# The router's logits with the weights held still, the last column block's idle products, and the end of the last norm, in a Hymba block on one core

## The chip, the core and the metric

The kernel runs on one core of a Trainium2 chip. The metric is the time of one execution in device microseconds (us). The core has TensorE (PE, with its weight load PEld), VectorE (DVE), ScalarE (ACT), GpSimd (POOL) and SyncE (SP), which issues most of the DMAs.

## What is computed

```python
def block(x, c, ...):                     # x: 512 tokens x 2048 columns
    shift, scale, gate, shift2, scale2, gate2 = split(silu(c) @ w_ada + b_ada)
    h  = rmsnorm(x) * (1 + scale) + shift
    oa, ob = swa_attention(h @ w_in), fox_attention(h @ w_in)
    x1 = x + gate * (concat(rmsnorm(oa), rmsnorm(ob)) @ w_out)
    h2 = rmsnorm(x1) * (1 + scale2) + shift2
    logits = h2 @ [w_group | w_expert]    # 4 groups and 32 experts: 36 columns
    # top-1 of 4 groups, then top-2 of the 8 experts of that group
    x2 = x1 + gate2 * moe(h2)
    return rmsnorm(x2, final_g)
```

Products that decide the router are made in full fp32, or as three products of split halves (hi*hi, lo*hi, hi*lo).

## The kernel before

The tokens are four blocks of 128 (`tb`). The part that the change touches first is the output projection. x1 is made in four blocks of 512 columns, `cc`, in the order 2, 0, 1, 3. For a block, 16 pieces of w_out (512 KB each; two of one kind in `n`, `j`) are loaded by SP (L360) into a ring of five buffers named `raw`; ACT rounds a piece to `hi_s` (L175), DVE makes the remainder `lo_s` (L176), and PE does for each half piece twelve products into four accumulators `oq` (L214 to L216, three for each token block). The first loop over `cc` has slots only for half pieces 4 to 6, block 3 for all; the last piece of a block is done in `out_last`, token block by token block, with DVE's `gx` and `x` after each (L1108, L1109: x1 = x + gate * accumulator).

Beside it runs `ada_side`: four sections of w_ada for the last gate (`gm`), eight loads of 512 KB each, in the same `raw` ring, with the same SP queue. Half of a section's tiles go through DVE (`ga`, L621), half through ACT (L623, scales the buffer in place) and POOL (L624, adds it to `gb`). Its steps are written out at a fixed rate, 66 for 26 half pieces.

The third thing between output products is the `Tail` of a block that is done. For a token block it is a T step (`tr`: four transposes of x1 into PSUM, `x1T`, L1123; ACT squares x1 for the norm, L1116, and copies x1T to `x1Ts`, L1127) and an L step (`logit`: four fp32 products with x1Ts held and the 36 router columns `wr` streamed, L1132, each two PE instructions, and one DVE operation that adds the result `lp` to `lg`, L1134 and L1136). `steps()` yields T and L in turn, eight steps for a block; the loop takes one step after each half piece with `next(steps, 0)`. There are 24 steps for the blocks 2, 0 and 1, and 23 slots; the rest is done before the last piece. PSUM tag `t`, in which x1T, lp and `gr` (the ada side's transposed result, L596) live, has two buffers.

The last block, 3, has its T and L steps in `out_last` and after it, on a PSUM tile of its own (`lp4`). Then DVE adds lg and lp4 (L1199), multiplies by the norm's factor rs (L1211), adds the bias (L1212), and a chain of some twenty small operations chooses groups and experts, up to `chosen_b` (L1253). In that time PE does `turn(22)`, 22 products of the identity with itself into a tile that nobody reads (L1229, fp32, two instructions each); then `rk` (ranks, L1257), `turn(8)`, and the gather `xe` (L1499) of the first expert pair, whose DVE and ACT work follows (L1480, L1486, L1506, L1508). 16 expert pairs follow, 1024 KB of weights a load.

The end is `last_norm`: the squares of x2, by five chunks of columns (four of them 512, 512, 512, 256 and the last 256 wide) for each token block, on ACT (L1605) into `sf5`; DVE reduces (L1608), scales (L1609), takes the inverse root with ACT's help (L130 to L134), and writes the output in eight halves of 1024 columns (L1616), each sent by SP (L1617).

Of the kernel before, what the change touches and what calls it, by code (L numbers as in the profile page):

```python
# [8 lines left out]
F32 = mybir.dt.float32  # L9
# [3 lines left out]
AF = mybir.ActivationFunctionType  # L13
OP = mybir.AluOpType
AX = mybir.AxisListType

T = 512
D = 2048
TB = 4
EPS = 1e-6  # L20
# [33 lines left out]
def kernel(  # L54
# [8 lines left out]
    V, S, G, PE, SP = nc.vector, nc.scalar, nc.gpsimd, nc.tensor, nc.sync  # L63
# [8 lines left out]
    def bcast(v, n):  # L72
        return bass.AP(tensor=v.tensor, offset=v.offset, ap=[[0, 128], [1, n]])
# [5 lines left out]
    def flat(t):  # L79
        return t.rearrange("p a b -> p (a b)")  # L80
# [18 lines left out]
    ident = big.tile([128, 128], F32, name="ident")  # L99
# [408 lines left out]
    def bank(shape, name):  # L508

        return pb["pool"].tile(shape, F32, tag=pb["tag"], name=name, bufs=pb["bufs"])  # L510
# [328 lines left out]
    def side_step():  # L839
        f = side_late.pop(0) if side_late else None  # L840
        if f:
            f()

    def attend(segs):


        us = [(u, i) for i, sg in enumerate(segs) for u in sg[0]]
        counts = [sum(1 for _, j in us if j == i) for i in range(len(segs))]
        late, at = None, -1
        for k in range(len(us) + LAG):  # L850
            u, i = us[k] if k < len(us) else (None, len(segs) - 1)
            if i != at:
                if at >= 0:
                    fill.drain()
                at = i
                _, make, total, hook = segs[i]
                fill = make()
                step = total / (2.0 * counts[i] + (2.0 * LAG if i == len(segs) - 1 else 0.0))
                if hook:
                    hook(fill)  # L860
                if u.pre:
                    u.pre()
                    fill.take(1.3)
            if u:
                u.a1()
            if 0 < k <= len(us):
                us[k - 1][0].a2()
            fill.take(step)
            if late:
                late()  # L870
                late = None
            if k >= LAG:
                us[k - LAG][0].b()
                late = us[k - LAG][0].c
            fill.take(step)
            if k + 1 < len(us) and us[k + 1][1] == at and us[k + 1][0].pre:
                us[k + 1][0].pre()
            else:
                side_step()
        late()  # L880
        return fill
# [19 lines left out]
    for g in range(4):  # L901
        VP += natural(256, lambda g=g: accs("accv", f"vb{g}"),
                      lambda tb, o, g=g: S.activation(vbs[g][:, tb, :], o, AF.Copy))

    def fills(i):
        for kind, n, *to in FILLS[i]:
            if kind == "v":
                for v in VP[n:to[0]]:
                    yield from v
            else:  # L910
                yield from (queries2 if kind == "q" else heads2)(n)
# [84 lines left out]
    wrf = wr.rearrange("p c j e -> p (c j) e")  # L996
# [27 lines left out]
    def more_o(fill):  # L1024
# [3 lines left out]
    total = lambda i: 2.56 * sum(to[0] - n if to else 8 for _, n, *to in FILLS[i])  # L1028
    last6 = list(fox_units((6,), qks, vbs))
    f = attend([  # L1030
        (swa_units(((0, 2), (1, 3), (4, 6), (5, 7))[i]) if i < 4 else
         fox_units((i - 4,), qks, vbs) if i < 10 else last6[:LAST], lambda i=i: Fill(fills(i), side, RATE), total(i),
         hooks.get(i))
        for i in range(11)
    ] + [(last6[LAST:] + list(fox_units((7,), qks, vbs)), lambda: Fill(out_first()), LAST_FILL, router)])
# [20 lines left out]
    mo = ctx.enter_context(tc.tile_pool(name="mo", bufs=1, reuse_waits="tile"))  # L1056
    gm = mo.tile([128, D], F32, name="gm")
    ss2 = mo.tile([128, TB, 4], F32, name="ss2")
    lg = mo.tile([128, TB, 36], F32, name="lg")

    def sm(shape, name, dt=F32):
        return mo.tile(shape, dt, name=name)

    def bc(t, shape):
        return t.to_broadcast(shape)

    rs = sm([128, TB], "rs")
# [23 lines left out]
    class Tail:  # L1091
# [35 lines left out]
            S.activation(self.xT[tb], t, AF.Copy)  # L1127

        def logit(self, tb):
            lp = self.lp4[:, tb, :] if self.last else bank([128, 36], f"lp_{self.cc}_{tb}")  # L1130
            for j in range(4):
                PE.matmul(lp, self.xT[tb][:, j, :], wrf[:, self.cc * 4 + j, :], start=j == 0, stop=j == 3)  # L1132
            if self.cc == 2:
                V.tensor_copy(lg[:, tb, :], lp)  # L1134
            elif not self.last:
                V.tensor_add(lg[:, tb, :], lg[:, tb, :], lp)  # L1136

        def steps(self):
            for tb in range(TB):
                self.tr(tb)  # L1140
                yield
                self.logit(tb)
                yield

    def out_last(t):
# [16 lines left out]
    tail = Tail(2, oacc[2])  # L1162
# [3 lines left out]
    for cc, first in ((0, 4), (1, 4), (3, 0)):  # L1166
        steps = chain(steps, tail.steps())
        ops = []
        for i in range(4):
            k = bank6 % 6  # L1170
# [3 lines left out]
        tail = Tail(cc, ops)  # L1174
# [21 lines left out]
    tail.logit(2)  # L1196
    rms_x1()
    tail.logit(3)
    V.tensor_add(lg, lg, tail.lp4)  # L1199
    pst.close()  # L1200
    frt.close()

# [5 lines left out]
    pb["pool"], pb["tag"], pb["bufs"], hold[0] = ps, "y", 4, True  # L1208
    while side_late:
        side_step()  # L1210
    V.tensor_mul(lg, lg, bc(rs[:, :, None], [128, TB, 36]))  # L1211
    V.tensor_add(lg, lg, bc(brt[:, None, :], [128, TB, 36]))  # L1212

    def one_hot(v, n, mx_, name):
# [11 lines left out]
    def turn(n):  # L1226

        for _ in range(n):
            PE.matmul(idle[:, :128], ident, ident, start=True, stop=True)  # L1229

    turn(22)
    gl = lg[:, :, 0:4]
    gmax = sm([128, TB], "gmax")
    V.tensor_reduce(gmax, gl, axis=AX.X, op=OP.max)
# [20 lines left out]
    for tb in range(TB):  # L1255
        for k in range(tb + 1):
            PE.matmul(rk[:, tb, :], before if k == tb else ones_b, chosen_b[:, k].rearrange("p g e -> p (g e)"),  # L1257
                      start=k == 0, stop=k == tb)
    turn(8)
    place = sm([128, TB, 4, 8], "place")  # L1260
    pf = place.rearrange("p t g e -> p t (g e)")
    V.scalar_tensor_tensor(place, chosen_b, FAR, bc(off.rearrange("p a b e -> p (a b) e")[:, None], [128, TB, 4, 8]),
                           op0=OP.mult, op1=OP.add)
# [19 lines left out]
    HID = cw[:, 5120:5632]  # L1283
# [4 lines left out]
    YT = [cw[:, 5632:6144], more_f[:, 1, :], big.tile([128, 512], F32, tag="wr", name="yt2"), HID]  # L1288
# [225 lines left out]
    def total(tb):  # L1514

        if not x2s:
            x2s.extend(rp_.tile([128, D], F32, tag=f"x2{i}", name=f"x2_{i}") for i in range(TB))
        return x2s[tb]
# [77 lines left out]
    sf5 = sm([128, TB, 5], "sf5")  # L1596
    sf, rf, tf = sm([128, TB], "sf"), sm([128, TB], "rf"), sm([128, TB], "tf")

    def last_norm(cols, tb=0):
        if cols is None:  # L1600
            SP.dma_start(fg, bcast(final_g, D))
            return
        c0, c1 = cols
        i = CHUNKS.index(cols)
        S.activation(HID[:, :c1 - c0], total(tb)[:, c0:c1], AF.Square, accum_out=sf5[:, tb, i:i + 1])  # L1605
        if c1 < D or tb < 3:
            return
        V.tensor_reduce(sf, sf5, axis=AX.X, op=OP.add)  # L1608
        V.tensor_scalar(sf, sf, 1.0 / D, EPS, op0=OP.mult, op1=OP.add)  # L1609
        rsqrt_(rf, sf, tf)  # L1610
        for tb in range(TB):
            y = ring_tile()
            for h in range(2):
                sl = slice(h * 1024, (h + 1) * 1024)
                yv = flat(y)[:, sl]
                V.scalar_tensor_tensor(yv, total(tb)[:, sl], rf[:, tb:tb + 1], fg[:, sl], op0=OP.mult, op1=OP.mult)  # L1616
                SP.dma_start(out[tb * 128:(tb + 1) * 128, sl], yv)  # L1617
# [113 lines left out]
```

## Time and profile before

| | |
|---|---|
| runs of the kernel before | 1891.93, 1893.37, 1896.53 us; median 1893.37 |
| the profiled execution | 1895.8 us; span in the trace 1893.9 us |
| PE busy | 1810.1 us, 96% of the span |
| DVE, ACT, POOL busy | 1018.6, 748.7, 288.2 us |
| DMA | 573.84 MB, mean 303 GB/s |

The span is cut by the trace: output projection 768 to 891 us, router 891 to 906, expert pairs to 1868, end to 1893.9. In the trace "PE L216 MATMUL oq" is line 216 on TensorE writing the tile oq; "[0.38 <-DVE chosen_b]" is idle time before an instruction and what ended it; PEclk is the granted TensorE clock as a share of full speed (1.00 is 2.4 GHz, 0.50 is 1.2 GHz).

### The profile page before, as it was taken

What the parts mean: (1) busy time and instruction counts of PE and PEld (TensorE: products, weight loads), DVE (VectorE), ACT (ScalarE), POOL (GpSimd) and SP (SyncE); (2) the same over time, 40 slices, a digit from 0 to 9 for tenths busy, and PEclk for the clock granted to TensorE, in tenths of its full rate; (3) what the DMA queues carried; (4) which work ended last, traced back from release to release, by engine and by line L of the source; (5) the groups of instructions that cost most, each with busy time, mean ns of one, the idle gap of its engine ahead of it and who ended that gap; (6) DMA issues with size and microseconds to landing.
All of it is one profiled execution on the core that took longest, in us unless ns stands there. A gap on an engine that the chain in (4) does not pass through costs nothing.

```text
span 1893.9 us, 26581 instructions
## 1 busy us (share of the span) xinstructions
PE 1810.1 (96%) x10045; PEld 1131.1 (60%) x10045; DVE 1018.6 (54%) x1812; ACT 748.7 (40%) x1462; POOL 288.2 (15%) x217
## 2 busy tenths in 40 slices
PE   7998999899899999999999999999999999999995
PEld 5668887787787777778544454444444444444432
DVE  4334676666566545757555454544554545545435
ACT  3235656565555443345523233232322323323213
POOL 0000434443354321445000000000000000000000
PEclk8998999999999999999999999999999999999998
DMA  9984555565566342668989999999999999999995
GB/s 338 352 274 106 169 164 152 165 196 173 160 186 186 113 142 78 208 214 295 369 344 397 420 419 421 421 420 420 420 418 421 416 420 420 419 420 416 420 413 215
DMA packets 208791, 573.84 MB, mean 303 GB/s; under 512 B 22624, under 2 KB 110728, under 8 KB 159888
## 3 DMA queue, kind: packets, MB, share of 16 engines
q1 hardware_dynamic: 207744, 572.00, 80.3%
q8 instruction: 81, 1.33, 0.3%
q14 instruction: 54, 0.44, 0.1%
q10 hardware_dynamic: 912, 0.07, 0.0%
HBM read 567.82 MB, written 4.19 MB: 302 GB/s over the span
## 4 chain that ended last, share of the span: by engine, by line
PE 74%; DMA 8%; ACT 7%; DVE 7%; issue 3%; POOL 1%; SPq 0%; DVEq 0%; ACTq 0%; POOLq 0%
PE pu L1363 12%; PE pg L1363 11%; PE y L1385 9%; PE xe L1499 7%; PE o L1407 5%; DMA w<-in_w_up_dram 4%; PE qp L214 3%; PE qp L216 3%; PE qp L215 3%; DMA raw<-in_w_ada_dram 2%; PE gv L325 2%; PE acc L214 1%; PE acc L215 1%; PE acc L216 1%; PE ob L826 1%
## 5 line engine op out<-in xcount | busy, mean ns | idle before, releaser
L1363 PE MATMUL pu<-w,cw 128*64 128x512 f32 x1024 | 239.3, 593 | 4.7 <-DMA w<-in_w_up_dram 4.7
L1363 PE MATMUL pg<-w,cw 128*64 128x512 f32 x1024 | 235.5, 598 | 1.3 <-ACT cw L1508 0.8
L1508 ACT ACTIVATE cw<-xe,shM,scM 128x128 f32<-128x128 f32 x128 | 58.5, 458 | 429.2 <-PE xe L1499 396.2
L1385 PE MATMUL y<-w,more_f 128*64 128x512 f32 x960 | 214.2, 598 | 4.1 <-ACT xp_whi L1480 2.3
L1506 DVE TENSOR_SCALAR cw<-xe,scM,shM 128x128 f32<-128x128 f32 x128 | 52.4, 410 | 299.3 <-ACT cw L1508 299.3
L624 POOL TENSOR_TENSOR gb<-gb,raw 128x512 f32<-128x512 f32 x112 | 162.1, 1448 | 275.8 <-ACT raw L623 211.4
L1410 DVE SCALAR_TENSOR_TENSOR x<-o,wpair,x 128x512 f32<-128x512 f32 x240 | 163.2, 743 | 19.3 <-PE o L1407 19.3
L1363 PEld LDWEIGHTS pu<-w,cw 128*64 128x64 f32 x1024 | 76.0, 137 | 154.1 <-issue 140.3
L1480 ACT ACTIVATE xp_whi<-x,rs 128x256 fp32r<-128x256 f32 x236 | 162.6, 762 | 0.9 <-DVE rs L134 0.9
L1385 PEld LDWEIGHTS y<-w,more_f 128*64 128x64 f32 x960 | 71.2, 137 | 134.4 <-issue 111.1
L1363 PEld LDWEIGHTS pg<-w,cw 128*64 128x64 f32 x1024 | 69.7, 136 | 133.5 <-issue 128.4
L176 DVE TENSOR_TENSOR wlo_s<-raw,whi_s 128x512 fp32r<-128x512 f32 x96 | 91.4, 953 | 107.7 <-ACT whi_s L175 107.6
L1486 DVE SCALAR_TENSOR_TENSOR xp_wlo<-x,rs,xp_whi 128x256 fp32r<-128x256 f32 x232 | 144.8, 681 | 2.2 <-ACT xp_whi L1480 2.2
L621 DVE SCALAR_TENSOR_TENSOR ga<-raw,csil,ga 128x512 f32<-128x512 f32 x112 | 111.3, 994 | 26.2 <-DMA raw<-in_w_ada_dram 25.6
L1499 PE MATMUL xe<-cr,xp_whi 128*128 128x256 f32 x472 | 120.5, 294 | 0.0
L1499 PEld LDWEIGHTS xe<-cr,xp_whi 128*128 128x128 f32 x472 | 88.7, 188 | 47.3 <-issue 45.4
L1499 PE MATMUL xe<-cr,xp_wlo 128*128 128x256 f32 x472 | 114.3, 281 | 0.0
L214 PE MATMUL qp<-hT_hi,whi_s 128*128 128x512 f32 x256 | 107.3, 419 | 0.0
L216 PE MATMUL qp<-hT_hi,wlo_s 128*128 128x512 f32 x256 | 101.2, 395 | 0.0
L215 PE MATMUL qp<-hT_lo,whi_s 128*128 128x512 f32 x256 | 101.2, 395 | 0.0
L623 ACT ACTIVATE raw<-raw,csil 128x512 f32<-128x512 f32 x112 | 79.8, 713 | 34.0 <-DMA raw<-in_w_ada_dram 32.7
L1499 PEld LDWEIGHTS xe<-cr,xp_wlo 128*128 128x128 f32 x472 | 88.9, 188 | 0.0
(445 smaller groups left out, 3372.5 us busy)
## 6 DMA issues: line engine op xcount, KB each, us to landing
w<-in_w_gate_dram SPq DMA_DIRECT2D x128, 1024.0 KB, 10.6
w<-in_w_up_dram SPq DMA_DIRECT2D x128, 1024.0 KB, 13.9
w<-in_w_down_dram SPq DMA_DIRECT2D x126, 1024.0 KB, 10.3
raw<-in_w_ada_dram SPq DMA_DIRECT2D x128, 512.0 KB, 4.2
raws<-in_w_ada_dram SPq DMA_DIRECT2D x64, 512.0 KB, 8.9
raw<-in_w_in_dram SPq DMA_DIRECT2D x160, 128.0 KB, 2.8
raw<-in_w_out_dram SPq DMA_DIRECT2D x32, 512.0 KB, 3.8
raw<-in_w_in_dram SPq DMA_DIRECT2D x48, 256.0 KB, 3.3
```

The costliest lines, as they stand in the source:

```text
L214: PE.matmul(o, lhi, rhi, start=first, stop=False, **kw)
L215: PE.matmul(o, lhi, rlo, start=False, stop=False, **kw)
L216: PE.matmul(o, llo, rhi, start=False, stop=last, **kw)
L621: V.scalar_tensor_tensor(a, ts[n][:, j, :], s, a, op0=OP.mult, op1=OP.add)
L624: G.tensor_add(a, a, ts[n][:, j, :])
L1363: PE.matmul(o[64 * e:64 * e + 64, :], self.xe(cc)[:, j, 64 * e:64 * e + 64], w[cc, e][:, j, :], start=cc == 0 and j == 0, stop=cc == 3 and ...
L1385: PE.matmul(ys[dc][64 * e:64 * e + 64, :], HT[:, k, 64 * e:64 * e + 64], self.wd[k, e][:, dc, :], start=k == 0, stop=k == 3)
L1407: PE.matmul(o, self.ohT[:, tb, :], v, start=i == 0, stop=i == 1)
L1410: V.scalar_tensor_tensor(x2, o, self.w_col(tb), x2 if self.n else x1[dc][:, tb, :], op0=OP.mult, op1=OP.add)
L1480: S.activation(hi[tb], xv, AF.Identity, scale=s)
L1486: V.scalar_tensor_tensor(lo[tb], xv, s, hi[tb].bitcast(F32), op0=OP.mult, op1=OP.subtract)
L1499: PE.matmul(t[:, j, :], v[tb][:, j, :], OHS[:, tb].rearrange("p q s -> p (q s)"), start=tb + i == 0, stop=tb + i == TB)
```

## The change

- The logits of blocks 2, 0 and 1 are made the other way round: `wr` (36 columns) is held and x1Ts (128 columns) streamed, two of the four products to rows 0 to 35 of lp and two to rows 64 to 99; DVE adds both halves to a transposed sum `lgT`. For block 3 the products stand as before, and one more, lgT times two stacked identities (`both`), brings the sum over.
- `steps()` puts the transposes of a token block and the logits of the one ahead of it in one step: five steps for a block.
- The add of lg and lp4 and the multiplication by rs become one DVE operation.
- The idle products: 15 and 6 for 22 and 8.
- The end: the squares of the last chunk of token blocks 2 and 3 go to DVE; POOL sums the first four chunks and scales them, DVE adds the last one in one operation; the last output half is sent as 640 and 384 columns.

```diff
--- before.py
+++ after.py
@@ -1058,6 +1058,13 @@
     ss2 = mo.tile([128, TB, 4], F32, name="ss2")
     lg = mo.tile([128, TB, 36], F32, name="lg")
 
+    lgT = mo.tile([128, T], F32, name="lgT")
+    G.memset(lgT, 0.0)
+    both = mo.tile([128, 36], F32, name="both")
+    G.memset(both, 0.0)
+    for e in (0, 64):
+        G.tensor_copy(both[e:e + 36, :], ident[e:e + 36, e:e + 36])
+
     def sm(shape, name, dt=F32):
         return mo.tile(shape, dt, name=name)
 
@@ -1127,19 +1134,30 @@
             S.activation(self.xT[tb], t, AF.Copy)
 
         def logit(self, tb):
-            lp = self.lp4[:, tb, :] if self.last else bank([128, 36], f"lp_{self.cc}_{tb}")
+            sl = slice(tb * 128, (tb + 1) * 128)
+            if self.last:
+                lp = self.lp4[:, tb, :]
+                PE.matmul(lp, lgT[:, sl], both, start=True, stop=False)
+                for j in range(4):
+                    PE.matmul(lp, self.xT[tb][:, j, :], wrf[:, self.cc * 4 + j, :], start=False, stop=j == 3)
+                return
+            lp = bank([128, 128], f"lp_{self.cc}_{tb}")
             for j in range(4):
-                PE.matmul(lp, self.xT[tb][:, j, :], wrf[:, self.cc * 4 + j, :], start=j == 0, stop=j == 3)
-            if self.cc == 2:
-                V.tensor_copy(lg[:, tb, :], lp)
-            elif not self.last:
-                V.tensor_add(lg[:, tb, :], lg[:, tb, :], lp)
+                e = 64 * (j % 2)
+                PE.matmul(lp[e:e + 36, :], wrf[:, self.cc * 4 + j, :], self.xT[tb][:, j, :], start=j < 2, stop=j > 1)
+            for e in (0, 64):
+                o = lgT[e:e + 36, sl]
+                if self.cc == 2:
+                    V.tensor_copy(o, lp[e:e + 36, :])
+                else:
+                    V.tensor_add(o, o, lp[e:e + 36, :])
 
         def steps(self):
-            for tb in range(TB):
-                self.tr(tb)
-                yield
-                self.logit(tb)
+            for tb in range(TB + 1):
+                if tb < TB:
+                    self.tr(tb)
+                if tb:
+                    self.logit(tb - 1)
                 yield
 
     def out_last(t):
@@ -1196,7 +1214,7 @@
     tail.logit(2)
     rms_x1()
     tail.logit(3)
-    V.tensor_add(lg, lg, tail.lp4)
+    V.tensor_mul(lg, tail.lp4, bc(rs[:, :, None], [128, TB, 36]))
     pst.close()
     frt.close()
 
@@ -1208,7 +1226,6 @@
     pb["pool"], pb["tag"], pb["bufs"], hold[0] = ps, "y", 4, True
     while side_late:
         side_step()
-    V.tensor_mul(lg, lg, bc(rs[:, :, None], [128, TB, 36]))
     V.tensor_add(lg, lg, bc(brt[:, None, :], [128, TB, 36]))
 
     def one_hot(v, n, mx_, name):
@@ -1228,7 +1245,7 @@
         for _ in range(n):
             PE.matmul(idle[:, :128], ident, ident, start=True, stop=True)
 
-    turn(22)
+    turn(15)
     gl = lg[:, :, 0:4]
     gmax = sm([128, TB], "gmax")
     V.tensor_reduce(gmax, gl, axis=AX.X, op=OP.max)
@@ -1256,7 +1273,7 @@
         for k in range(tb + 1):
             PE.matmul(rk[:, tb, :], before if k == tb else ones_b, chosen_b[:, k].rearrange("p g e -> p (g e)"),
                       start=k == 0, stop=k == tb)
-    turn(8)
+    turn(6)
     place = sm([128, TB, 4, 8], "place")
     pf = place.rearrange("p t g e -> p t (g e)")
     V.scalar_tensor_tensor(place, chosen_b, FAR, bc(off.rearrange("p a b e -> p (a b) e")[:, None], [128, TB, 4, 8]),
@@ -1602,16 +1619,25 @@
             return
         c0, c1 = cols
         i = CHUNKS.index(cols)
-        S.activation(HID[:, :c1 - c0], total(tb)[:, c0:c1], AF.Square, accum_out=sf5[:, tb, i:i + 1])
+        v = total(tb)[:, c0:c1]
+        if c1 == D and tb > 1:
+            V.tensor_tensor_reduce(YT[1][:, :c1 - c0], v, v, scale=1.0,
+                                   scalar=0.0, op0=OP.mult, op1=OP.add, accum_out=sf5[:, tb, i:i + 1])
+        else:
+            S.activation(HID[:, :c1 - c0], v, AF.Square, accum_out=sf5[:, tb, i:i + 1])
+        if i == 3 and tb == 3:
+
+            for k in range(1, 4):
+                G.tensor_add(sf, sf5[:, :, 0] if k == 1 else sf, sf5[:, :, k])
+            G.tensor_scalar(sf, sf, 1.0 / D, EPS, op0=OP.mult, op1=OP.add)
         if c1 < D or tb < 3:
             return
-        V.tensor_reduce(sf, sf5, axis=AX.X, op=OP.add)
-        V.tensor_scalar(sf, sf, 1.0 / D, EPS, op0=OP.mult, op1=OP.add)
+        V.scalar_tensor_tensor(sf, sf5[:, :, 4], 1.0 / D, sf, op0=OP.mult, op1=OP.add)
         rsqrt_(rf, sf, tf)
         for tb in range(TB):
             y = ring_tile()
-            for h in range(2):
-                sl = slice(h * 1024, (h + 1) * 1024)
+            for c0, c1 in ((0, 1024), (1024, 2048)) if tb < 3 else ((0, 1024), (1024, 1664), (1664, 2048)):
+                sl = slice(c0, c1)
                 yv = flat(y)[:, sl]
                 V.scalar_tensor_tensor(yv, total(tb)[:, sl], rf[:, tb:tb + 1], fg[:, sl], op0=OP.mult, op1=OP.mult)
                 SP.dma_start(out[tb * 128:(tb + 1) * 128, sl], yv)
```

On PE, the end of the last half piece with a slot and the start of the piece behind it, in block 3's loop (rows of before; oq are block 3's accumulators, x1T_3 and lp_3 belong to block 1's last token block):

```order
L215 MATMUL oq_3_7755<-lo_s_8051,mx_hi 128x512
L216 MATMUL oq_3_7755<-hi_s_8050,mx_lo_6446 128x512
L1123 MATMUL x1T_3_8144<-ident,x_1_6599 128x128 [waits PE_49]
L1123 MATMUL x1T_3_8144<-ident,x_1_6599 128x128 x3
L1132 MATMUL lp_3_8156<-wr,x1Ts_3_8149 128x36 [waits DVE_49,Activation_49]
L1132 MATMUL lp_3_8156<-wr,x1Ts_3_8149 128x36 x3
L214 MATMUL oq_0_7752<-hi_s_8104,mx_hi 128x512
L215 MATMUL oq_0_7752<-lo_s_8105,mx_hi 128x512
```

The same place on PE in the changed kernel:

```order
L215 MATMUL oq_3_7811<-lo_s_8103,mx_hi 128x512
L216 MATMUL oq_3_7811<-hi_s_8102,mx_lo_6446 128x512
L214 MATMUL oq_0_7808<-hi_s_8142,mx_hi 128x512 [waits Activation_49]
L215 MATMUL oq_0_7808<-lo_s_8143,mx_hi 128x512 [waits DVE_49]
L216 MATMUL oq_0_7808<-hi_s_8142,mx_lo_6446 128x512
```

The T and L steps between the last pieces are gone from here; block 1's last L stands eight half pieces earlier.

On ACT, from the first T step of block 2 in the loop of block 0 (rows of before; L623 are the ada side's, x1Ts_1 is block 2's second token block):

```order
L1127 ACTIVATE x1Ts_0_7374<-x1T_0_7369 128x512
L623 ACTIVATE raw<-raw,csil 128x512
L175 ACTIVATE hi_s_7387<-raw 128x1024
L623 ACTIVATE raw<-raw,csil 128x512
L1116 ACTIVATE x1Ts_1_7431,ss_7268<-x_2_7259 128x512
L1127 ACTIVATE x1Ts_1_7431<-x1T_1_7426 128x512
L623 ACTIVATE raw<-raw,csil 128x512 x2
```

The same place in the changed kernel:

```order
L1134 ACTIVATE x1Ts_0_7380<-x1T_0_7375 128x512
L623 ACTIVATE raw<-raw,csil 128x512
L175 ACTIVATE hi_s_7393<-raw 128x1024
L1123 ACTIVATE x1Ts_1_7414,ss_7268<-x_2_7259 128x512
L1134 ACTIVATE x1Ts_1_7414<-x1T_1_7409 128x512
L623 ACTIVATE raw<-raw,csil 128x512
L1123 ACTIVATE x1Ts_2_7446,ss_7268<-x_2_7259 128x512
L1134 ACTIVATE x1Ts_2_7446<-x1T_2_7441 128x512
L623 ACTIVATE raw<-raw,csil 128x512 x2
```

The second L623 stood ahead of x1Ts_1's square and copy, and now stands behind both.

On DVE, at the end, the last chunk's sums of x2 and what follows (rows of before):

```order
L1446 SCALAR_TENSOR_TENSOR x_2_8983<-o_1792_2_14154,wpair,x_2_8983 128x256
L1446 SCALAR_TENSOR_TENSOR x_3_8984<-o_1792_3_14155,wpair,x_3_8984 128x256
L1608 TENSOR_REDUCE sf<-sf_8365 128x4
L1609 TENSOR_SCALAR sf<-sf 128x4
L131 RECIPROCAL rf<-tf 128x4
```

The same place in the changed kernel (ISA is a sum of squares, and the read of its result):

```order
L1463 SCALAR_TENSOR_TENSOR x_2_8995<-o_1792_2_14170,wpair,x_2_8995 128x256
L1624 ISA more_f,sf_8377<-x_2_8995 128x256
L1624 ISA sf_8377 128x1
L1463 SCALAR_TENSOR_TENSOR x_3_8996<-o_1792_3_14171,wpair,x_3_8996 128x256
L1624 ISA more_f,sf_8377<-x_3_8996 128x256
L1624 ISA sf_8377 128x1
L1635 SCALAR_TENSOR_TENSOR sf<-sf_8377,sf 128x4
L131 RECIPROCAL rf<-tf 128x4
```

Two sums of squares have come in, one of them between the adds of x_2 and x_3; the reduction and the scaling have become one operation.

## Rows read from the trace of the kernel before

**Rows 1.** Windows: us, busy time and instructions of each engine, PEclk, DMA share, GB/s

```profile
768.00:831.00 63.00, 59.31 (x282) 47.75 (x281) 41.18 (x50) 24.77 (x40) 29.36 (x18) 1.00 0.67 221
...
870.00:891.00 21.00, 19.81 (x116) 17.05 (x117) 15.30 (x26) 8.86 (x19) 8.06 (x6) 1.00 0.84 304
```

**Rows 2.** Groups of instructions, 768 to 891 us: busy, mean ns | idle before, releaser

```profile
L624 POOL TENSOR_TENSOR gb<-gb,raw 128x512 f32<-128x512 f32 x28 | 43.7, 1560 | 40.0 <-ACT raw L623 39.5
L621 DVE SCALAR_TENSOR_TENSOR ga<-raw,csil,ga 128x512 f32<-128x512 f32 x28 | 32.3, 1154 | 25.3 <-DMA raw<-in_w_ada_dram 25.2
```

**Rows 3.** The chain that ended last, 760 to 930 us: start, us, what

```profile
774.74 0.60 ACT x1Ts L1127
...
831.62 0.51 PE oq L215
...
835.25 0.95 PE gr L596 x2
...
870.01 0.50 PE oq L215
...
911.08 3.58 PE pu L1363 x16
```

**Rows 4.** PE's timeline, 870 to 900 us: start, us, instruction, idle before

```profile
872.66 0.97 PE L1132 MATMUL lp<-wr,x1Ts 128*128 128x36 f32 x8
873.47 0.48 PE L214 MATMUL oq<-hi_s,mx_hi 128*128 128x512 f32 x1
...
876.33 0.63 PE L1123 MATMUL x1T<-ident,x 128*128 128x128 f32 x4
877.71 1.08 PE L1132 MATMUL lp<-wr,x1Ts 128*128 128x36 f32 x8 [0.75 <-ACT x1Ts L1127]
878.62 0.48 PE L214 MATMUL oq<-hi_s,mx_hi 128*128 128x512 f32 x1
...
892.46 5.07 PE L1229 MATMUL idle<-ident 128*128 128x128 f32 x44
897.91 0.19 PE L1257 MATMUL rk<-chosen_b,before 128*128 128x32 bf16 x1 [0.38 <-DVE chosen_b L1253]
```

**Rows 5.** DVE's timeline, 866 to 900 us

```profile
874.56 2.47 DVE L621 SCALAR_TENSOR_TENSOR ga<-raw,csil,ga 128x512 f32<-128x512 f32 x2
...
879.13 0.59 DVE L1193 TENSOR_SCALAR ss<-ss 128x4 f32<-128x4 f32 x1
880.30 0.69 DVE L1108 TENSOR_TENSOR gx<-oq,ga 128x512 f32<-128x512 f32 x1 [0.58 <-PE oq L216]
...
888.17 0.69 DVE L1114 CUSTOM_DVE_ANT_0 gx<-x 128x512 f32<-128x512 f32 x1
...
891.20 0.31 DVE L1211 TENSOR_TENSOR lg<-lg,rs 128x144 f32<-128x144 f32 x1
```

**Rows 6.** ACT's timeline, 770 to 800 us

```profile
776.80 0.71 ACT L623 ACTIVATE raw<-raw,csil 128x512 f32<-128x512 f32 x1
...
781.66 0.60 ACT L1127 ACTIVATE x1Ts<-x1T 128x512 f32<-128x512 f32 x1 [3.54 <-PE x1T L1123]
```

**Rows 7.** Windows with the granted clock, later in the kernel

```profile
947.00:949.60 2.60, 0.67 (x6) 0.43 (x6) 1.84 (x13) 0.91 (x3) 0.00 (x0) 1.00 1.02 429
...
951.00:953.00 2.00, 2.00 (x8) 0.70 (x6) 0.00 (x0) 0.00 (x0) 0.00 (x0) 0.50 1.02 430
```

**Rows 8.** The end: DVE's timeline from 1868 us

```profile
1869.24 3.22 DVE L1446 SCALAR_TENSOR_TENSOR x<-o,wpair,x 128x256 f32<-128x256 f32 x8
1874.45 0.17 DVE L1608 TENSOR_REDUCE sf<-sf 128x4 f32<-128x20 f32 x1 [2.00 <-ACT cw L1605]
...
1875.90 9.65 DVE L1616 SCALAR_TENSOR_TENSOR w<-x,rf,cw 128x1024 f32<-128x1024 f32 x8
```

**Rows 9.** The end: ACT's timeline from 1868 us

```profile
1872.07 0.18 ACT L1605 ACTIVATION_READ_ACCUMULATOR cw<-x 128x1 f32 x1
...
1874.23 0.19 ACT L1605 ACTIVATION_READ_ACCUMULATOR cw<-x 128x1 f32 x1
```

## The prediction

> **What bounds the kernel now.** I read the page first: PE is busy for 96% of the span, so the question is in which stretches it is PE that makes the others wait. The windows over the stages come second [rows 1]. In the output projection, 768 to 831 us, PE is busy 59.31 of 63 us, DVE 41.18 and ACT 24.77, at DMA share 0.67 and granted clock 1.00; from 870 to 891 us PE is busy 19.81 of 21. This alone looks like a stretch in which every PE instruction counts. The groups of the stretch say something else [rows 2]: DVE's L621 waits 25.2 us in sum for loads of w_ada, and POOL's L624 39.5 us for ACT's L623. PE is nearly full, and loads, ACT, POOL and DVE are a ring that runs beside it.
>
> The chain of waits decides between the two [rows 3]. It leaves PE with ACT's copy at 774.74 and comes back to PE only at 831.62, through loads of w_ada, L623, L624 and lo_s; it stays on PE until the two gr that end near 836.2, leaves again, and is on PE from 870.01. So before 870 a product saved on PE mostly makes PE wait longer for the next lo_s; from 870 to the router it counts. PE's and DVE's timelines for that last part [rows 4, 5] are where the sum is made.
>
> **The change, part by part.**
>
> *The logits of blocks 2, 0 and 1.* An L step is 0.81 us now (872.66 to 873.47 [rows 4]). No row shows the new form: 36 columns held, 128 streamed, in two column groups. A plain 128x128 fp32 instruction is the idle product: 5.07 us for 44, 115 ns each [rows 4]. What halves of the array save is shown by pu, which streams 512 columns through 64-column halves: 3.58 us for 16, 224 ns each, against gr, 512 columns through the whole array, 0.95 us for 2, 475 ns [rows 3]. That is 0.47, so a new instruction is between 54 ns (the halves overlap) and 115 ns (they don't), and eight of them 0.43 or 0.92 us. I take 0.43, since pu is the nearest row. The gain is 0.38 us for each of the ten L steps before 870, 3.8 us in all, of which I count only the one in the stretch where the chain is on PE (831.62 to 836.2): **-0.4 us**. The cover of the other nine is the wait for lo_s; if that cover is gone they are worth 3.4 us more.
> A rule speaks against the low price. The Trainium skill, "TensorE: Matmul & The Clock Gate", Part 3, has a weight load overlap with products in flight only where the row group differs, and both halves here use all 128 rows. By that rule the eight cost 0.92 us and their loads besides, and this term is nothing or a small loss rather than -0.4. The trace's 224 ns against 475 has the same full row group in both halves and does not agree with it.
>
> DVE pays: 24 operations of 36x128 (near the 0.31 us of a 128x144 one [rows 5]) for 12 of about 0.18, some 5 us more over 100 us. Its wait of 25.2 us for loads [rows 2] covers them; I count nothing.
>
> *T and L together.* Fifteen steps rather than 24 are used up by the fifth slot of block 3's loop, so the T and L steps that stand behind 870 are gone from there. On PE that is L from 872.66 to 873.47, 0.81; then T, the wait of 0.75 us for ACT's copy, and L, all from 876.33 to 878.62, 2.29 [rows 4]: 3.10 us together. PE could have the accumulator for gx at 880.30 - 3.10 = 877.2. But DVE is the later one now: its two L621 end at 874.56 + 2.47 = 877.03, and behind them stand two operations on ss, the second of 0.59 (879.13), about 0.75 us together, so gx starts at about 877.8 and not at 880.30 [rows 5]: **-2.5 us**. Bounds: nothing, if DVE's loads come later by as much, and -3.1. SP's queue has its loads in the same order.
>
> *The last block's extra product and the joined operation.* lgT times `both` is two instructions of 115 ns [rows 4] in four places. One stands ahead of the products for the last gx, the others behind each other in the tail where DVE waits for the last logits: between 0.2 and 0.9, I take +0.5. The joined DVE operation saves 0.31 [rows 5]. Net **+0.2 us**.
>
> *The idle products.* They start with the router chain, 2.5 us earlier, near 889.9, and 30 instructions at 115 ns end at 893.4. chosen_b comes 2.7 us (0.4 + 2.5 - 0.2) before its old 897.9, near 895.2. PE idles about 1.8 us there instead of 0.38 [rows 4]. At a clock that stays up this costs nothing, since DVE's chain is what `rk` waits for.
>
> *The end.* ACT's last square is read at 1874.42, and DVE's reduction waits for it until 1874.45 [rows 8, 9]. The squares follow each other by 0.54 (four from 1872.07 to 1874.23 [rows 9]), so without two of them ACT is done at 1873.34. DVE's adds end at 1869.24 + 3.22 = 1872.46 [rows 8]; two sums of squares of 256 columns come on top. The row is 0.69 for 512 columns [rows 5], so 256 are between half of it, 0.35, and 0.69; I take 0.43, a little over half for the reading of the result: 1873.3. Both meet at 1873.4. From there to the output it took 1.45 us (1874.45 to 1875.90 [rows 8]), and one operation of about 0.21 is saved: output from 1874.6, 1.3 earlier. The last send is 384 columns of 1024. At the 429 GB/s of [rows 7] a send of 512 KB moves for 1.22 us, so the shorter one is worth between nothing and 0.76, less the extra operation; I take 0.2. Together **-1.5 us**, bounds -0.6 and -2.2. POOL must have its sum ready at 1873.4: two of its four operations come behind the square of chunk 3, read at 1872.25 [rows 9]. A POOL operation of 128x4 has no row here; it lies between DVE's 0.17 [rows 8] and POOL's 1.56 for 128x512 [rows 2]. I take the low end, with 128 times fewer elements: ready at 1872.6.
>
> *What lies between*, the expert pairs, starts from what the router gives and is shifted as a whole.
>
> Sum: -0.4 - 2.5 + 0.2 - 1.5 = -4.2 us. The profiled execution of 1895.8 us would be 1891.6; it lies 2.4 above the median of the runs, and from the median 1893.37 the forecast is **1889.2 us**.
>
> **Rivals.**
>
> *PE is the bound all the way* (faster). For it: 59.31 us of 63 busy [rows 1]. Against: 57 us of the chain off PE [rows 3]. Then the other nine L steps count too: -4.2 - 3.4 = -7.6, 1885.8 us.
>
> *The ring slips* (slower). The change puts an L623 behind a T step's square and copy on ACT. The one at 776.80 [rows 6] would start behind the second T step, whose transposes PE begins near 777.26 (its copy then stood at 781.66 [rows 6]): 777.3 + 0.5 for the transposes + 0.6 for the copy, about 778.3; POOL has its earlier operation until then, so its next one is about 1.1 us later, and so is the load that takes the buffer. One such slip that is not made up takes 1.1 us: -3.1, 1890.3. There are twelve T steps in the loops. If nine slipped by 1.1 each, the sum would be +5.7, 1899.1; from four on, the gain is gone. For it: L624's 39.5 us of waits on L623 [rows 2]. Against: the copies stood in ACT's queue before too, and a DMA share of 0.67 [rows 1] leaves room to catch up.
>
> *The clock falls in PE's longer wait.* At 947 to 949.6 PE was busy for 0.67 us of 2.6 and the clock was 0.50 from 951 to 953 [rows 7]. A wait of 1.8 us and a shorter turn behind it are of that kind. `rk` waits for DVE, so only what is left of the low clock at the first pu and pg counts, at half speed: some 3 us of low clock cost 1.5. Sum -2.7, 1890.7 us.
> The Trainium skill, same page, "Why this matters for your kernels", asks for no idle gaps between bursts of products, and its gap is longer than mine. By that rule alone the clock stays and the sum is -4.2. The row fell after less, so the trace does not quite agree, and the rival keeps a chance.
>
> *POOL is late at the end.* At 1.56 us each, POOL's two operations end at 1875.4; DVE then starts its output 0.7 us later than before, rather than 1.3 earlier. Sum -4.2 + 2.0 = -2.2, 1891.2 us.
>
> *The middle brings nothing* because the loads behind 870 follow the ring: only the end is left, -1.5, 1891.9 us.
>
> **How the numbers follow.** Forecast with its own bounds (1887 to 1891): 0.44. PE bound: 0.18. One slip: 0.10. Clock: 0.08. POOL late: 0.05. Only the end: 0.08. The ring slips throughout: 0.07. About 0.3% (5.7 us) is what a measurement of this kernel can tell from no change; faster than that begins at 1887.7. To it belong the PE rival, 0.18, and a third of the forecast's 0.44, where both ends come out well: 0.32. Slower needs nearly the whole ring to slip, 0.07. The rest is 0.61. The range goes from 1884, below the PE rival and its bounds, to 1894.5, which holds the smaller rivals and a few slips.
>
> **What would show it.** Right: L's eight instructions in about 0.45 us; no T or L on PE between 870 and gx; gx about 2.5 us earlier against the first lo_s of the last piece; PE idle 1.5 to 2 us ahead of `rk` at clock 1.00; the output 1.2 us sooner behind the last o. Wrong: lo_s of the last pieces coming at another time than before (ring); a clock below 1.00 between 893 and 910; POOL's sums ending behind 1873.4, or their like.

## The result and the profile after

The changed kernel takes 1883.97 us (median of 6 runs, 1881.39 to 1887.32), the kernel before on the same chip 1892.84 (6 runs, 1891.72 to 1896.53): ratio 0.9946, interval 0.9929 to 0.9964. The forecast was 1889.2, its range 1884.0 to 1894.5. The time lies at the lower edge, just outside, and the gain is 8.9 us where 4.2 were forecast. Of the runs below, the profiled executions of e_end and e_logit took 4028 and 5391 us, far from every timed one, and no row is taken from them.

The windows of the kernel after, in the columns of [rows 1]:

```profile
831.00:870.00 39.00, 34.36 (x168) 25.76 (x166) 22.26 (x26) 17.17 (x28) 24.52 (x17) 1.00 0.68 224
870.00:891.00 21.00, 20.36 (x106) 16.99 (x107) 16.69 (x26) 8.82 (x18) 8.82 (x6) 0.92 0.89 339
...
1100.00:1800.00 700.00, 696.05 (x3480) 332.18 (x3478) 355.38 (x590) 209.15 (x349) 0.00 (x0) 1.00 1.01 424
```

The last row is one that the prediction never asked for: the expert pairs, whose code is the same in both kernels. Their loads run at 424 GB/s. The kernel before, profiled again as c_before, has in the same window:

```profile
1100.00:1800.00 700.00, 694.52 (x3456) 328.07 (x3454) 352.01 (x586) 207.98 (x347) 0.00 (x0) 1.00 1.01 419
```

The DMA share is 1.01 in both: the DMA engines never rest. PE is busy for 99% of the window too, so the rows alone don't tell which of the two sets the pace; the experiments with pads below do, since they change nothing on PE and move the time. The pairs are measured from the first pg to the last x. Both ends in c_before:

```profile
904.88 1.08 PE L1363 MATMUL pg<-w,cw 128*64 128x512 f32 x4
...
1869.16 3.21 DVE L1446 SCALAR_TENSOR_TENSOR x<-o,wpair,x 128x256 f32<-128x256 f32 x8
```

And the first pg of the kernel after (its last x stands further below):

```profile
903.23 1.08 PE L1380 MATMUL pg<-w,cw 128*64 128x512 f32 x4
```

That is 967.5 us in c_before (904.88 to 1872.37) and 959.3 in the kernel after (903.23 to 1862.52): 8.2 us less, nearly the whole gain of 8.9 in the medians. The first pg is 904.29 in the profile before and 903.23 after, 1.1 us earlier, not 2.7.

PE's timeline of the kernel after, around the last pieces and the router:

```profile
870.43 0.51 PE L215 MATMUL oq<-lo_s,mx_hi 128*128 128x512 f32 x1 [2.26 <-DVE lo_s L176]
...
872.19 0.63 PE L215 MATMUL oq<-lo_s,mx_hi 128*128 128x512 f32 x1
872.62 0.63 PE L216 MATMUL oq<-hi_s,mx_lo 128*128 128x512 f32 x1
...
876.03 0.40 PE L214 MATMUL oq<-hi_s,mx_hi 128*128 128x512 f32 x1
876.26 0.39 PE L215 MATMUL oq<-lo_s,mx_hi 128*128 128x512 f32 x1
...
891.71 3.51 PE L1246 MATMUL idle<-ident 128*128 128x128 f32 x30
896.84 0.19 PE L1274 MATMUL rk<-chosen_b,before 128*128 128x32 bf16 x1 [1.61 <-DVE chosen_b L1270]
```

Up to the last product of the last piece no T or L step stands here any more. In its place PE waits 2.26 us for lo_s, and then runs for some 3 us with a product every 0.43 us instead of 0.23. The window of that stretch:

```profile
871.80:874.80 3.00, 3.00 (x9) 2.33 (x8) 2.96 (x3) 1.75 (x3) 1.69 (x2) 0.50 1.04 368
```

The granted clock is 0.50, the lower of its two levels. DVE's rows that answer to [rows 5]:

```profile
879.00 0.69 DVE L1115 TENSOR_TENSOR gx<-oq,ga 128x512 f32<-128x512 f32 x1 [0.33 <-PE oq L216]
...
890.12 0.31 DVE L1217 TENSOR_TENSOR lg<-lp,rs 128x144 f32<-128x144 f32 x1 [0.61 <-PE lp L1142]
```

The end, DVE's timeline (answering to [rows 8]):

```profile
1862.04 0.48 DVE L1463 SCALAR_TENSOR_TENSOR x<-o,wpair,x 128x256 f32<-128x256 f32 x1
...
1863.13 0.17 DVE L1635 SCALAR_TENSOR_TENSOR sf<-sf,sf 128x4 f32<-128x4 f32 x1
...
1864.37 9.79 DVE L1642 SCALAR_TENSOR_TENSOR w<-x,rf,cw 128x1024 f32<-128x1024 f32 x9
```

From the last x (1862.52) to the output it is 1.85 us, where it was 3.44 [rows 8].

### The profile page after: what moved, and what is told of

The parts are those of the page before. It is cut to its first block, busy times and chain, and to the rows that moved or that the text cites. A ratio compares the mean times of both kernels' runs of the same rounds, so it can differ in the third digit from the quotient of the medians.

```text
span 1882.8 us, 26578 instructions
## 1 busy us (share of the span) xinstructions
PE 1801.5 (96%) x10035; PEld 1129.6 (60%) x10035; DVE 1026.5 (55%) x1827; ACT 748.0 (40%) x1458; POOL 287.9 (15%) x225
## 4 chain that ended last, share of the span: by engine, by line
PE 78%; DVE 8%; ACT 6%; DMA 5%; issue 3%; POOL 0%; SPq 0%; DVEq 0%; ACTq 0%; POOLq 0%
PE pu L1380 12%; PE pg L1380 11%; PE y L1402 10%; PE xe L1516 7%; PE o L1424 5%; DMA w<-in_w_up_dram 3%; PE qp L214 3%; PE qp L216 3%; PE qp L215 2%; PE gv L325 2%; PE acc L214 1%; DMA raw<-in_w_ada_dram 1%; PE acc L215 1%; PE acc L216 1%; PE ob L826 1%
## 5 line engine op out<-in xcount | busy, mean ns | idle before, releaser
L621 DVE SCALAR_TENSOR_TENSOR ga<-raw,csil,ga 128x512 f32<-128x512 f32 x112 | 110.4, 986 | 13.1 <-DMA raw<-in_w_ada_dram 12.5
L215 PE MATMUL qp<-hT_lo,whi_s 128*128 128x512 f32 x256 | 101.2, 395 | 0.0
L623 ACT ACTIVATE raw<-raw,csil 128x512 f32<-128x512 f32 x112 | 79.6, 713 | 27.9 <-DMA raw<-in_w_ada_dram 27.6
```

What stands on the lines that cost most here:

```text
L215: PE.matmul(o, lhi, rlo, start=False, stop=False, **kw)
L621: V.scalar_tensor_tensor(a, ts[n][:, j, :], s, a, op0=OP.mult, op1=OP.add)
```

## The experiments

All ratios are to the kernel before on the same chip, with 95% intervals. First the parts one by one, and the kernel before itself.

**c_before**: no edit. 

> The kernel before, unchanged, profiled beside the parts. If the rate of the weight loads between 1100 and 1800 us (420 GB/s before, 424 after) belongs to the kernel, it is 420 again and the ratio 1.000; if it belongs to the chip or the hour of the first two profiles, this profile shows another rate, for example 424, with the same time as the other runs of the kernel before.


Measured: 1893.49 us, 0.9995 (0.9984 to 1.0005), 419 GB/s. The rate belongs to the kernel and not to the hour of the first profiles.

**e_end**: the hunk on `last_norm` alone. 

> Only the new end of the last norm. Theory of local gains: -1.3 us at the output's start, expert pairs as long as before, ratio 0.9993. Theory of the rate (the expert pairs' loads run at 420 or 424 GB/s, set when the stage fills up near 1030 us): nothing ahead of 1860 us is changed, so the rate is 420 and the ratio again 0.9993; if the rate is 424 here, it is no effect of the router part.


Measured: 1891.85 us, 0.9996 (0.9979 to 1.0014). No 8 us come from the end; -1.3 can't be told from nothing here.

**e_turn**:

```diff
-    turn(22)
+    turn(15)
...
-    turn(8)
+    turn(6)
```

> Only 15 and 6 idle products for 22 and 8. Local gains: 0.0 us, since rk waits for DVE; ratio 1.000. Rate: if the state of the loads is set by what PE does between 892 and 905 us, the rate becomes 424 and the time falls by 7 to 9 us; if not, 1.000.


Measured: 1894.17 us, 1.0001 (0.9992 to 1.0011), 419 GB/s: no gain, and no loss, as forecast.

**e_logit**: all but the end and the turns. 

> The transposed logits, the joined steps and the joined DVE operation, with 22 and 8 idle products and the old end. Local gains: -1 to -3 us (the first product of the expert pairs came 1.05 us earlier with the whole change), ratio 0.9985 to 0.9995. Rate: if this part sets the state, the loads run at 424 GB/s and the time falls by 8 to 10 us, ratio 0.995; without it about -1.


Measured: 1886.59 us, 0.9953 (0.9939 to 0.9966). So the gain comes with this part. For the rate:

**e_logit2**: the same once more. 

> The same kernel as e_logit, for a profile: expert pairs' loads at 424 GB/s if the rate is where its gain of 0.5% lies, at 420 if it lies ahead of 1030 us.


Measured: 1886.54 us (one run), 423 GB/s between 1100 and 1800 us. The gain is in the rate.

Then that part was taken apart.

**e_steps**: the hunk on `steps` alone. 

> Only the order of the steps: transposes of a token block and logits of the one ahead placed together, five steps for a block, logits and all else as before. Local gains: the T and L steps behind 870 us are gone, -2 us at the first expert product, ratio 0.999. Rate: if the order is what sets the loads' state, 424 GB/s and a ratio of 0.995 to 0.996.


Measured: 1894.05 us, 1.0007 (0.9998 to 1.0016), 419 GB/s. The order of the steps does not bring it.

**e_tlog**: the hunks on `logit`, lgT, both and the joined operation, with the old `steps`. 

> Only the transposed logits and the joined DVE operation, with the eight steps for a block as before. Local gains: about 0 (L is 0.25 us shorter on TensorE for the two behind 870 us, the extra products cost 0.15 each), ratio 0.9995 to 1.0005. Rate: if the tiles or the logits set the loads' state, 424 GB/s and 0.995 to 0.996.


Measured: 1884.78 us, 0.9950 (0.9936 to 0.9964), 424 GB/s. So it is in these hunks, which hold the new tiles as well as the new products.

**e_alloc**: the kernel before with nothing but this, and no reader of it:

```diff
+    lgT = mo.tile([128, T], F32, name="lgT")
+    G.memset(lgT, 0.0)
+    both = mo.tile([128, 36], F32, name="both")
+    G.memset(both, 0.0)
+    for e in (0, 64):
+        G.tensor_copy(both[e:e + 36, :], ident[e:e + 36, e:e + 36])
```

> The kernel before with the two new tiles made and filled by GpSimd (lgT and both), and read by nobody. If the place of the tiles behind them in SBUF sets the rate of the expert pairs' loads, 424 GB/s and a ratio near 0.995; by every other theory 1.000 and 420 GB/s.


Measured: 1885.97 us, 0.9955 (0.9942 to 0.9969). Its window:

```profile
1100.00:1800.00 700.00, 696.10 (x3486) 329.28 (x3484) 356.15 (x592) 208.95 (x349) 0.00 (x0) 1.00 1.01 423
```

Two tiles that nobody reads bring the gain. They take 2208 bytes of each partition in the pool `mo`, and what comes behind them moves up. Among it are four of the twelve buffers into which SP loads the expert weights (8192 bytes a partition each): in the program's allocation they start at byte 128096 before, at 130304 in e_alloc and in the changed kernel. The other eight, in the pool `wring`, start at 163808 + 8192 k in both. Four of those eight take part only in the first loads and then hold x2, so between 1100 and 1800 us eight buffers are in use, four in each pool, in turn.

So the next kernels move these buffers, with little else: behind the four in `mo` stand only eleven small tiles, which move with them (a_all moves the eight in `wring` instead). A pad is one tile that GpSimd fills and nobody reads:

```diff
     sf, rf, tf = sm([128, TB], "sf"), sm([128, TB], "rf"), sm([128, TB], "tf")
+    pad = mo.tile([128, 8], F32, name="pad")
+    G.memset(pad, 0.0)
```

**e_pad32**: the kernel before with this pad of 8 words, 32 bytes. 

> The kernel before with one unread tile of 32 bytes a partition ahead of the four weight buffers w that lie in the pool mo: they start at byte 128128 of a partition, a multiple of 64, rather than at 128096. Nothing else is moved but some small tiles behind them. Theory of alignment (a load into a buffer that starts 32 bytes off a multiple of 64 is slower): 424 GB/s between 1100 and 1800 us and a ratio of 0.995. Theory of distance (the large shift by 2208 bytes matters, or GpSimd's fills): 420 and 1.000.


Measured: 1894.07 us, 1.0001 (0.9991 to 1.0012), 419 GB/s.

**e_pad64**: 16 words. 

> The same with 64 bytes: the buffers start at 128160, again 32 off a multiple of 64. Alignment: 420 GB/s and 1.000. If any shift helps: 424 and 0.995.


Measured: 1894.87 us, 1.0007 (0.9998 to 1.0017), 420 GB/s.

**a_back**: the changed kernel with the pad of 32 bytes. 

> The changed kernel with 32 bytes ahead of the same four buffers: they start at 130336, 32 off a multiple of 64 as before the change. Alignment: 420 GB/s, and what is left is the sum of the change's own parts, -2 to -4.2 us, ratio 0.998 to 0.999. If alignment isn't it: 424 and 0.995.


Measured: 1896.95 us, 1.0016 (1.0007 to 1.0025). Its window:

```profile
1100.00:1800.00 700.00, 692.66 (x3449) 327.97 (x3446) 352.25 (x586) 207.71 (x347) 0.00 (x0) 1.00 1.01 418
```

32 bytes ahead of four buffers cost the changed kernel some 13 us (1.0016 against 0.9946), its whole gain and more: the pairs take 971.8 us here (902.98 to 1874.78), some 4 us more than with the other slow starts. But e_pad32 refutes the theory of 64 bytes: a multiple of 64, even of 128, gains nothing.

**a_all**: the changed kernel, and 32 bytes made last in `wring`, so that its eight buffers start at multiples of 64:

```diff
+    padded = []
...
     def last_norm(cols, tb=0):
         if cols is None:
+            if not padded:
+                padded.append(rp_.tile([128, 8], F32, name="padr"))
+                G.memset(padded[0], 0.0)
```

> The changed kernel with 32 bytes behind the eight other weight buffers, in the pool wring, so that all twelve start at a multiple of 64 (163776 rather than 163808 for the first of the eight). Alignment of each buffer for itself: the eight gain too, up to twice the first gain, 428 GB/s or more and a ratio of 0.985 to 0.99. If four aligned buffers already take the wait away: as the changed kernel, 0.995.


Measured: 1884.94 us, 0.9957 (0.9943 to 0.9970), 424 GB/s: as without.

The start that was quick so far, 130304, is a multiple of 256; 128096, 128128, 128160 and 130336 are not.

**e_pad160**: the pad with 40 words. 

> The kernel before with 160 unread bytes a partition ahead of the four weight buffers in mo: they start at 128256, a multiple of 256 (with 32 bytes it was a multiple of 128 but not of 256, and slow; the changed kernel's 130304 is a multiple of 256). If a start at a multiple of 256 is what counts: 423 to 424 GB/s and a ratio of 0.9955. If not: 420 and 1.000, and it is something else about 130304.


Measured: 1883.89 us, 0.9957 (0.9944 to 0.9970), 423 GB/s.

**e_pad2208**: 552 words. 

> The kernel before with 2208 unread bytes there: the four weight buffers start at 130304, exactly as in the changed kernel, while every tile ahead of them stays where it was. If the place of these buffers alone is the cause: 423 to 424 GB/s, 0.9955. If the shift of the other tiles (the ring of 2 KB tiles, lg, the router's small tiles) does it: 420 and 1.000.


Measured: 1884.11 us, 0.9957 (0.9944 to 0.9971), 424 GB/s. Every tile ahead of these buffers stays where it was in the kernel before, so it is their place that counts, and a multiple of 256 bytes is enough.

**e_256**: e_pad160, and the tile of a_all with 56 words, 224 bytes. 

> The kernel before with 160 bytes in mo and 224 behind the ring in wring: all twelve weight buffers start at multiples of 256. If each buffer gains by its own start: more than the changed kernel, 427 GB/s and a ratio of 0.991 to 0.993. If four are enough: 424 and 0.9955. If the multiple of 256 is not the cause: 420 and 1.000.


Measured: 1882.11 us, 0.9945 (0.9932 to 0.9958). Its window:

```profile
1100.00:1800.00 700.00, 697.74 (x3490) 328.65 (x3490) 357.36 (x593) 208.96 (x349) 0.00 (x0) 1.00 1.01 425
```

Counted from the DMA records of the traces, for the 8192-byte packets between 1100 and 1800 us (quartiles of a packet's time in ns, and the share of packets over 311):

```
kernel     start of mo's buffers,   quarter  median  three     over
           wring's, modulo 256                       quarters  311 ns
c_before    96, 224                 311      313     315       0.69
e_pad32    128, 224                 311      313     315       0.71
a_back      32, 224                 313      313     315       0.87
e_pad160     0, 224                 309      309     309       0.21
after        0, 224                 309      309     309       0.22
e_256        0,   0                 309      309     309       0.00
```

The packets counted are the weight loads' own, and it is they that get shorter; so the small tiles that moved beside the buffers are not the cause.

The last question was what the change's own parts are worth once the rate is the same.

**a_256**: the changed kernel with all twelve at multiples of 256. In `weights`:

```diff
-        gex = sm([128, TB, 4], "gex")
+        gex = rp_.tile([128, TB, 4], F32, name="gex")
...
-        gp = sm([128, TB, 2], "gp")
+        gp = rp_.tile([128, TB, 2], F32, name="gp")
```

and the same for gsum, gval, w2 and w1, together 224 bytes in `wring`. 

> The changed kernel with all twelve weight buffers at multiples of 256 bytes (six small tiles of the expert weights moved to the pool wring, 224 bytes, which shifts its eight buffers; the four in mo stay at 130304). Alignment, each buffer for itself: 425 GB/s as in e_256. The change's own parts come on top of it: e_256 less 1.1 us for the end, and 0 to -2 for the router part: 1880 to 1881 us, ratio 0.993 to 0.994.


Measured: 1882.37 us, 0.9940 (0.9927 to 0.9953), 425 GB/s.

**e_256b**: e_256 again, beside it. 

> e_256 again beside a_256, so that the change's own parts are measured with the loads at the same rate in both: ratio 0.9945 as before; a_256 below it by 1 to 3 us.


Measured: 1880.71 us, 0.9926 (0.9914 to 0.9938), 425 GB/s. The kernel before with 384 bytes of padding is the fastest version that was run; the change on top of it adds nothing that can be measured (the intervals overlap, and the medians lie 1.7 us the wrong way).

**a_256s**: a_256 with the order in the half piece turned round:

```diff
+                due += 66 / 26.0
+                while due >= 1:
+                    due -= 1
+                    next(side, None)
                 if n > first or j:
                     next(steps, 0)
                     if j == 0:
                         side_step()
-                due += 66 / 26.0
-                while due >= 1:
-                    due -= 1
-                    next(side, None)
```

> a_256 with the ada side's steps written out ahead of the T and L steps in each half piece, so that an L623 stands ahead of the T step's square and copy on ScalarE. Theory that the w_ada ring slips because L623 stands behind these copies (the last lo_s starts at 873 to 874.5 us in profiles of the changed order and at 868 to 873 in those of the old one): the last lo_s comes 1 to 3 us earlier and the time falls as much, ratio 0.992 to 0.993. Theory that the spread is chance: no difference from a_256.


Measured: 1888.71 us, 0.9968 (0.9958 to 0.9979), 6 us slower than a_256; the last lo_s starts at 877.99, not earlier but 6.6 us later than in a_256 (871.43). Putting L623 ahead of the copies is no cure, so that cause of the late lo_s is not shown. Nor is it ruled out: the edit moves the whole ada side, L621 on DVE as well, and L623's own wait for loads, from 768 to 891 us, grows from 29.3 us in a_256 to 49.4.

## Why the prediction was wrong

The step that failed: *"What lies between, the expert pairs, starts from what the router gives and is shifted as a whole."* The prediction gave the pairs no term and read no row for what sets their pace. From the first pg to the last x it is 959.2 us in the mean of six profiles with 423 or 424 GB/s (e_alloc, e_tlog, e_logit2, the kernel after, e_pad160, e_pad2208) and 967.8 in six with 419 or 420 (the two of the kernel before, e_turn, e_steps, e_pad32, e_pad64): 8.6 us. What did it is shown: four weight buffers that start at a multiple of 256 bytes. The diff shows two new tiles, but neither it nor the order of instructions tells what they move; the allocation does, and the prediction did not look at it.

The Trainium skill, "DMA: Bandwidth & Descriptors", section "How a descriptor splits into AXI transactions", has a rule of this kind, worded for reads: a transaction must start at a multiple of 256 bytes, so a descriptor that starts off one begins with a transaction from the boundary below it. By that rule an 8192-byte row off the boundary needs 33 transactions instead of 32, and by an estimate from the rule up to 319 ns instead of 309. In this case's traces the packets took 313 in the median instead of 309: the boundary and the direction agree, the size is less than a full transaction.

Between the rates, 425 GB/s against 420 is 1.2%. That the start in SBUF, where the load writes, is one that counts is shown by the runs, since the pads moved nothing in the tensors that the loads read. Why the slow starts differ among each other (0.87 of the packets over 311 ns at 32 bytes past the boundary in a_back, 0.69 to 0.71 in the two others that were counted) stays open.

The other steps, by their own terms:

- *A product saved before 870 makes PE wait longer for lo_s*: right. From 831 to 870 us PE is busy for 34.36 us, where it is 37.40 in the kernel before, by the cheaper L and by the steps that now stand earlier; the last lo_s came no sooner for it, and PE's waits for lo_s went from 3.8 us to 6.2. The rows of before, that window and the group of L215 from 768 to 891 us:

```profile
831.00:870.00 39.00, 37.40 (x188) 30.44 (x187) 22.39 (x25) 20.21 (x34) 25.84 (x17) 1.00 0.69 229
...
L215 PE MATMUL oq<-lo_s,mx_hi 128*128 128x512 f32 x128 | 50.9, 398 | 3.9 <-DVE lo_s L176 3.8
```

  The groups of the kernel after, 768 to 891 us:

```profile
L215 PE MATMUL oq<-lo_s,mx_hi 128*128 128x512 f32 x128 | 51.3, 401 | 6.2 <-DVE lo_s L176 6.2
...
L621 DVE SCALAR_TENSOR_TENSOR ga<-raw,csil,ga 128x512 f32<-128x512 f32 x28 | 32.3, 1155 | 12.4 <-DMA raw<-in_w_ada_dram 12.1
```

- *DVE pays some 5 us, and its wait for loads covers them*: right. lgT's 24 operations take 6.9 us where lg's 12 took 2.2, and L621's wait for loads fell from 25.2 us [rows 2] to 12.1, so cover was left.
- *The price of a transposed L*: 0.43 was taken. In the chain of the kernel after it is 0.56:

```profile
806.52 0.56 PE lp L1147 x8
```

  The halves overlap, though not wholly (0.92 was the other bound), so the saving is 0.25 for each L and not 0.38. By the rule that the prediction names from the Trainium skill ("TensorE: Matmul & The Clock Gate", Part 3) it would have been 0.92 and more, and the trace does not agree with that.
- *T and L behind 870, -2.5 us*: the mechanism is right, 5.5 us from the last lo_s to gx (mean of the kernel after, a_back, a_all, e_logit2 and a_256) where ten profiles of the old order have 7.5: -1.9. But the last lo_s starts 2.1 us later in these five (873.1 against 871.0), so gx comes at 878.6 against 878.4, and the first pg at 903.5 against 902.9. (e_steps and e_tlog, which have half of the change each, and a_256s are in neither group.) So the rival of the ring that slips came out in its effect, about two slips of 1.1 us; the cause that it gave is not shown (a_256s). The profiles of one order spread by 5 us here, so 2 us are little to build on, though on each of the three chips in the record with profiles of both orders the new one is later, by 1.1 to 2.9.
- *The extra product and the joined operation, +0.2*: from gx to lg 10.56 us before, 11.12 after (879.00 to 890.12), and one operation of 0.34 less: +0.2. In the means of the five and the ten profiles, from gx to the add of the bias behind it, it is 11.75 against 11.29: +0.5, more than this pair shows.
- *The idle products, nothing*: right. PE waited 1.61 us ahead of rk (1.8 forecast), the clock between 891 and 905 us was 1.00. It fell at another place, past 871 after the wait of 2.26 for lo_s, and cost some seven products 0.2 each, about 1.4 us ahead of gx. The rival of the clock had its fall behind 893, not here.
- *The end, -1.5*: the sum of token block 2 delays the last x by about 0.45, and the output starts 1.6 earlier behind that: -1.1, where 1.3 was forecast. POOL's sum was ready at 1862.5, before DVE's 1863.13; that rival fell. But the shorter last send cost rather than gave. From the output's start to the end of the span it is 18.4, 18.7 and 18.7 us in the kernel after, a_back and a_256, and 18.0, 18.2, 17.7 and 17.6 in the profile before, c_before, e_pad160 and e_256b: +0.7. Its landing, kernel after:

```profile
out_dram<-w SPq DMA_DIRECT2D x7, 512.0 KB, 3.3
...
out_dram<-w SPq DMA_DIRECT2D x1, 192.0 KB, 4.1
```

  The last column is from issue to landing: 192 KB take longer than 512 KB. But the 512 KB sends land later in these kernels too (3.3 to 3.5 us, against 2.7 to 3.1 with the old end), and no run has the split send alone, so what makes the 0.7 is not shown.

So the parts that the prediction summed to -4.2 are +0.6 at the first pg and -0.4 at the end, near nothing, and the whole gain has another source. The rival *PE is the bound all the way*, which gave 1885.8, would have come nearest to the time, and is refuted all the same: PE's work from 831 to 870 us fell by 3 us and the last lo_s came no sooner. That a rival lay near the time was luck.

## What to carry to other kernels

Where a stage is bound by loads, print the start addresses of the tiles that they write, of the kernel before and after: a tile added for another purpose can move them, and here a change of 1% in such a stage outweighed everything that was saved on the engines beside it. Put such buffers at multiples of 256 bytes on purpose; 384 bytes of padding in the kernel before were worth 0.55 and 0.74% in two measurements. And ask of each stage that a change does not touch what sets its pace, before taking it as shifted.

## What the runs showed of the hardware

- A load of 8192-byte rows runs at 418 to 420 GB/s when four of the eight buffers in use start 32, 96, 128 or 160 bytes past a multiple of 256 and the other four 224, at 423 to 424 when the first four start on it, and at 425 when all do. That four are nearly enough was not expected and is not explained: in that stretch half of the loads go to `wring`, off the boundary, and yet only 22% of the packets are over 311 ns. These come in bunches. Counted by eighths of a round of eight loads (1024 packets in order of their start, the mean of 35 rounds of the kernel after), the share over 311 ns is 0.75 and 0.69 in two eighths, 0.20 and 0.09 in two more and at most 0.02 in the other four. That fits four loads that each gain by their own start; which load went to which buffer the packets do not say, and a kernel with only `wring` on the boundary was not run.
- A start at a multiple of 64 or 128 bytes that is none of 256 gained nothing (e_pad32: 419 GB/s, 1.0001).
- TensorE's clock fell to its lower level for some 3 us after a wait of 2.26 us that followed dense products (0.50 from 871.8 to 874.8), and stayed up over a wait of 1.61 us behind the idle products (1.00 from 891 to 905).
